# Q1 of a Strassen down projection made in two halves, and its weight sum T1 given tiles of its own

## The chip, the cores and the metric

The kernel runs on one core of a Trainium2 chip. The metric is the device time of one execution in microseconds (us). Names of engines: PE is the tensor engine (PEld its weight loads), DVE the vector engine, ACT the scalar engine, POOL the engine GpSimd, SP the sync engine, which issues most of the loads.

## The reference

A trunk of two layers on 512 tokens of 1024 features. Each layer has a token mixer, a cross-attention and an MLP, each followed by a layer norm of `alpha * x + sublayer(x)`. The change lies in the MLP, whose hidden width is 4096:

```python
def sq_relu_mlp(x, w1, b1, w2, b2):
    return jnp.square(jax.nn.relu(x @ w1 + b1)) @ w2 + b2
...
x = layer_norm(ALPHA * x + sq_relu_mlp(x, mlp_w1[i], mlp_b1[i], mlp_w2[i], mlp_b2[i]),
               ln_g[i, 2], ln_b[i, 2])
```

All data are float32.

## The kernel before

**Three matmuls for one.** Every operand of a matmul is split in a high part (a cast by ACT) and a low part (source minus high part, by DVE). `mm3` then issues three matmuls: high by high (line 198), high by the low part of the right side (199), and the low part of the left by the high part of the right (200). The names end in `h` and `l`.

**Quarters.** The 4096 hidden features are done in four quarters q of 1024. For q = 0, 1, 2 `up_down` makes the hidden tiles m = 0 to 7 (`s`: two tiles of four K tiles each, 128 hidden features per K tile) and then the down projection into `x`. In names "01" is layer 0, quarter 1. Quarter 3 has no Strassen products and is not touched. In quarters 1 and 2 the first six hidden tiles come from `up_pair`, which itself works with Strassen products (tiles `up`, `ub`, `utb`, `uta`, `ud`; PSUM `ua`, `ub`, `uc`), and tiles 6 and 7 from `feat_tile`, as do all eight in quarter 0.

**The down projection** is a Strassen product (Winograd's form) of the hidden block matrix, a11, a21 (K tiles 0 to 3, tokens 0 to 255 and 256 to 511), a12, a22 (K tiles 4 to 7), with the weights b11, b12, b21, b22 (512 by 512 each). Seven products stand on PE in this order: `u` = a11·b11, `f` = Q1·T1, `m2` = a12·b21, then onto `u` Q2·T2 and Q3·T3, onto `f` Q4·b22, onto `u` a22·T4. Here Q1 = a21 − a22, Q2 = −(a11 − a21) − a22, and the T are sums of weight blocks. Each product is 24 matmuls: 2 token tiles × 4 K tiles × 3. `a21` and `a22` are overwritten, so Q1 must be made after all eight hidden tiles, as the code stands.

**Weights.** `load` brings a block as two tiles of 128x1024 (pool `rawd`, six tiles) by SP. `onto_w` adds another block from HBM onto such tiles with an accumulating DMA on POOL's queue. `weight_split` makes high and low parts in the pools `wh` and `wl` of five tiles each; a tile comes free when PE has done its last matmul with it. The same pools serve the up projection. `split` makes the parts of an activation block in the pool `hid`.

In the code before, one pair of tiles `b` holds first b11, then T1 = b11 + b12, then T2, then T4:

```python
b = load("b11", 0, 0)
w = weight_split(f"b11{n}", b)
onto_w(b, 1, 0)
product(u, L["M1"], w, True, onto(0, 0))
V.tensor_tensor(a21, a21, a22, ALU.subtract)
w = weight_split(f"t1{n}", b)
onto_w(b, 1, 2)
product(f, split(f"q1{n}", a21), w, True, onto(1, 1))
```

**What sets the order.** Each engine, and each queue of DMA issues (SP's and POOL's), works through its own list in order and stops at an instruction whose inputs or buffers are not ready. The lists are fixed when the program is built, from the order of the code and from the buffers of the pools; an instruction can stand far from its neighbours in the code.

Of the kernel before, what the change touches and what calls it, by code (L numbers as in the profile page):

```python
# [10 lines left out]
F32R = mybir.dt.float32r  # L11
AF = mybir.ActivationFunctionType
ALU = mybir.AluOpType
AX = mybir.AxisListType

P = 128
# [23 lines left out]
def f32(ap):  # L40
    return ap.bitcast(F32)
# [3 lines left out]
def trunk(ctx: ExitStack, tc: tile.TileContext, a: dict, out: bass.AP):  # L45
    nc = tc.nc
    V, A, G, T = nc.vector, nc.scalar, nc.gpsimd, nc.tensor
# [22 lines left out]
    scoped = {}  # L70
# [126 lines left out]
    def mm3(out_, l, r, start, stop, skip=False):  # L197
        T.matmul(out_, l[0], r[0], start=start, stop=False, skip_group_check=skip)  # L198
        T.matmul(out_, l[0], r[1], start=False, stop=False, skip_group_check=skip)  # L199
        T.matmul(out_, l[1], r[0], start=False, stop=stop, skip_group_check=skip)  # L200
        if later:
            tick(3 * max(r[0].shape[-1], 128) / 2400)
# [10 lines left out]
    def tok(t):  # L213
        return slice(t * P, (t + 1) * P)
# [125 lines left out]
    for q in range(4):  # L340
# [3 lines left out]
        for z in range(2):  # L344
            k = 2 * q + z
            ld(r[:, z], a["xT"][:, k])
            h, l = x0.k(k)
# [122 lines left out]
    for j, c in enumerate((5, 2, 6, 3, 7, None, None, None)):  # L470
# [4 lines left out]
        for q in range(2):  # L475
            h = 2 * hf + q
# [177 lines left out]
    for i in range(DEPTH):  # L654
# [120 lines left out]
        def split(name, src):  # L775

            h, l = [scoped["hid"].tile([P, 4, 256], F32R, tag="hid", name=f"{name}{p}") for p in "hl"]
            A.copy(h, src)
            V.tensor_tensor(l, src, f32(h), ALU.subtract)
            return h, l  # L780

        def weight_split(name, src):
            us = []
            for j, r in enumerate(src):
                h = wh_p.tile([P, WU], F32R, tag="wh", name=f"{name}h{j}")
                l = wl_p.tile([P, WU], F32R, tag="wl", name=f"{name}l{j}")
                A.copy(h, r)
                V.tensor_tensor(l, r, f32(h), ALU.subtract)  # L788
                us.append([z.rearrange("p (k m) -> p k m", m=512) for z in (h, l)])
            return us  # L790

        def product(ps, lhs, rhs, start, evac):

            for g in range(2):
                for k in range(4):
                    w = rhs[k // 2]
                    mm3(ps[g], tuple(z[:, k, tok(g)] for z in lhs), (w[0][:, k % 2], w[1][:, k % 2]), start=start and k == 0, stop=k == 3, skip=not start)
                evac(g, ps[g])
# [3 lines left out]
        def block(r, c):  # L802

            return xm.half(c, slice(256 * r, 256 * r + 256))

        def x_sums():


            def raw(r, c):
                z = scoped["hid"].tile([P, 4, 256], F32, tag="hid", name=f"xr{i}{r}{c}")  # L810
                h, l = block(r, c)
                V.tensor_tensor(z, f32(h), f32(l), ALU.add)
                return z

            def parts(name, src, pool_):
                if pool_ is act_p:
                    z = act_p.tile([P, 2, 4, 256], F32R, tag="act", name=f"x{name}{i}")
                    h, l = z[:, 0], z[:, 1]
                else:
                    h, l = [pool_.tile([P, 4, 256], F32R, tag="hid", name=f"x{name}{i}{p}") for p in "hl"]  # L820
                A.copy(h, src)
                V.tensor_tensor(l, src, f32(h), ALU.subtract)
                xq[name] = h, l

            r = {}

            def start():
                r[22], r[21] = raw(1, 1), raw(1, 0)

            def q3():  # L830
                r[11] = raw(0, 0)
                V.tensor_tensor(r[11], r[11], r[21], ALU.subtract)

            def q1():
                parts("q3", r[11], act_p)
                V.tensor_tensor(r[21], r[21], r[22], ALU.subtract)

            def q2():
                parts("q1", r[21], act_p)
                V.scalar_tensor_tensor(r[11], r[11], -1.0, r[22], ALU.mult, ALU.subtract)  # L840

            def q4():
                parts("q2", r[11], scoped["hid"])
                r[12] = raw(0, 1)

            def end():
                V.tensor_tensor(r[12], r[12], r[11], ALU.add)
                parts("q4", r[12], scoped["hid"])

            chain(3, 5, [start, q3, q1, q2, q4, end])  # L850
# [66 lines left out]
        def up_down(q, n):  # L917

            s = [act_p.tile([P, 4, S], F32, tag="act", name=f"s{n}{b}") for b in range(2)]

            def ev(m, ps):
                r = t2(f"r{n}{m}")
                A.activation(r, ps, AF.Relu, bias=b1[:, i, 8 * q + m : 8 * q + m + 1], scale=1.0)
                A.activation(s[m // 4][:, m % 4], r, AF.Square)

            first = 0  # L930
            if q == 0:
                feat_first(f"h{n}", 4, lambda m: a["w1"][i, m], xm, ev)
                first = 4
                assert not later
                b2 = raw_p.tile([P, D], F32, tag="raw", name=f"b2{i}")
                ld(b2, a["b2"][i : i + 1, :].broadcast_to([P, D]))
                for t in range(NT):
                    V.scalar_tensor_tensor(x[t], x[t], ALPHA, b2, ALU.mult, ALU.add)
            a11, a21 = s[0][:, :, :256], s[0][:, :, 256:]
            a12, a22 = s[1][:, :, :256], s[1][:, :, 256:]  # L940
            L, R = {}, {}

            def load(name, hf, j):
                z = [scoped["rawd"].tile([P, WU], F32, tag="rawd", name=f"{name}{n}{z}") for z in range(2)]
                for w in range(2):
                    ld(z[w], a["w2"][i, q, hf, j + w])
                return z

            def first_blocks():
                L["M1"] = split(f"a11{n}", a11)  # L950
                V.tensor_tensor(a11, a11, a21, ALU.subtract)
                L["M7"] = split(f"q3{n}", a11)

            if q == 0:
                first_blocks()
                x_sums()
            for m in range(first, KC, 2):
                if m // 2 in STRASSEN_UP[q]:
                    up_pair(q, m, n, s[m // 4])
                else:  # L960
                    for z in range(2):
                        ev(m + z, feat_tile(f"h{n}{m + z}", a["w1"][i, 8 * q + m + z], xm, aux_p, "aux"))
                        last_product()
                if m == 4 and first == 0:
                    first_blocks()

            def onto(row, hf, op=ALU.add):
                def evac(g, ps):
                    z = x[2 * row + g][:, hf_cols(hf)]
                    V.tensor_tensor(z, z, ps, op)  # L970

                return evac

            def banks(name, p, tag):
                return [p.tile([P, 512], F32, tag=tag, name=f"{name}{n}{g}") for g in range(2)]

            u, f, m2 = banks("u", acc_p, "acc"), banks("f", acc_p, "acc"), banks("m2", tmp_p, "tmp")
            def onto_w(z, hf, j):

                for w in range(2):  # L980
                    G.dma_start(z[w], a["w2"][i, q, hf, j + w], accum_op=ALU.add)  # L981

            b = load("b11", 0, 0)
            w = weight_split(f"b11{n}", b)
            onto_w(b, 1, 0)
            product(u, L["M1"], w, True, onto(0, 0))
            V.tensor_tensor(a21, a21, a22, ALU.subtract)
            w = weight_split(f"t1{n}", b)
            onto_w(b, 1, 2)
            product(f, split(f"q1{n}", a21), w, True, onto(1, 1))  # L990
            b21 = load("b21", 0, 2)
            l12 = split(f"a12{n}", a12)
            product(m2, l12, weight_split(f"b21{n}", b21), True, onto(0, 0))
            t3 = load("t3", 1, 0)
            onto_w(t3, 1, 2)
            V.scalar_tensor_tensor(a11, a11, -1.0, a22, ALU.mult, ALU.subtract)
            w = weight_split(f"t2{n}", b)
            onto_w(b, 0, 2)
            product(u, split(f"q2{n}", a11), w, False, onto(0, 1, ALU.subtract))
            product(u, L["M7"], weight_split(f"t3{n}", t3), False, onto(1, 1, ALU.subtract))  # L1000
            b22 = load("b22", 1, 2)
            V.tensor_tensor(a12, a12, a11, ALU.add)
            product(f, split(f"q4{n}", a12), weight_split(f"b22{n}", b22), False, onto(0, 1))
            product(u, split(f"a22{n}", a22), weight_split(f"t4{n}", b), False, onto(1, 0))
# [15 lines left out]
        for q in range(3, 4):  # L1020
            n = f"{i}{q}"
            hid = Act(f"h{n}")
# [95 lines left out]
```

## Time and profile before

| | us |
|---|---|
| three runs | 1203.59, 1208.24, 1210.43 (median 1208.24) |
| profiled execution, own time | 1205.39 |
| its span, first to last instruction | 1203.5 |
| PE busy | 1184.3 (98%) |
| DVE busy | 847.3 (70%) |
| ACT busy | 616.2 (51%) |

The profiled execution is one more execution, with the profiler on. "Busy" of PE includes overlapping matmuls, so it does not say that PE runs at its best; what a place costs is read from the start times of matmuls there. The granted clock is a share of 2.4 GHz: 1.00 is the upper level, and a value between 0.5 and 1 means that part of the stretch ran at 1.2 GHz.

### The profile page before, as it was taken

To read this page: it belongs to the slowest core of one execution; us is meant where nothing else is said; L and a number is where in the kernel's file an instruction comes from. 1 tells how busy PE (TensorE), PEld (TensorE's weight loads), DVE (VectorE), ACT (ScalarE), POOL (GpSimd) and SP (SyncE) were. 2 spreads that over 40 slices of the span, in tenths; PEclk is the share of its full clock that TensorE was granted. 3 is DMA by queue.
4 is the path that set the end of the run, shared out by engine and by line. 5 is a ranking of instruction groups with operands and counts; after the bars stand their busy time and mean duration, and the time that the engine had idled before them with its cause. 6 is when DMAs were issued, how large, how long until landed. Compare 5 with 4: busy or idle time off the path is not lost.

```text
span 1203.5 us, 16624 instructions
## 1 busy us (share of the span) xinstructions
PE 1184.3 (98%) x6537; PEld 1027.5 (85%) x6537; DVE 847.3 (70%) x1173; ACT 616.2 (51%) x912; POOL 61.1 (5%) x99
## 2 busy tenths in 40 slices
PE   9999999999999999999999999999999999999997
PEld 7888898889889879879888889998987988978886
DVE  6774466585549798597775599775979869767336
ACT  6585774234423655656646434562365574654530
POOL 0211000000000000100100000000000010010000
PEclk9999999999999999999999999999999999999999
DMA  7344258633172643936745355637364583764311
GB/s 273 91 137 121 88 158 268 203 108 96 61 210 88 141 88 129 217 78 214 171 117 198 123 193 193 191 90 210 93 135 88 167 200 71 227 143 105 104 53 70
DMA packets 50974, 171.83 MB, mean 143 GB/s; under 512 B 6336, under 2 KB 6604, under 8 KB 50896
## 3 DMA queue, kind: packets, MB, share of 16 engines
q1 hardware_dynamic: 42960, 142.96, 36.6%
q0 software_dynamic: 7936, 27.81, 13.3%
q8 instruction: 51, 0.84, 0.3%
q14 instruction: 27, 0.22, 0.1%
HBM read 164.43 MB, written 6.31 MB: 142 GB/s over the span
## 4 chain that ended last, share of the span: by engine, by line
PE 82%; DVE 7%; DMA 4%; ACT 3%; issue 3%; POOL 0%; DVEq 0%; POOLq 0%; ACTq 0%; SPq 0%
PE h L198 5%; PE h L199 5%; PE h L200 5%; PE m L198 3%; PE m L199 3%; PE m L200 3%; PE u L198 3%; PE u L199 3%; PE u L200 3%; PE ao L200 2%; PE ao L198 2%; PE ao L199 2%; PE f L200 2%; PE q L199 2%; PE q L198 2%
## 5 line engine op out<-in xcount | busy, mean ns | idle before, releaser
L162 DVE TENSOR_TENSOR wl<-raw,wh 128x1024 fp32r<-128x1024 f32 x151 | 184.1, 1221 | 152.5 <-ACT wh L161 150.4
L161 ACT CAST wh<-raw 128x1024 fp32r<-128x1024 f32 x151 | 157.9, 1048 | 220.6 <-PE h L199 51.8
L981 POOL DMA_DIRECT2D b<-in_w x36 | 31.6, 879 | 281.0 <-DVE b1100l L788 62.3
L981 POOL DMA_DIRECT2D t<-in_w x12 | 10.7, 942 | 644.4 <-DMA t<-in_w 415.9
L249 ACT ACTIVATE rs<-mv,eps_t 128x1 f32<-128x1 f32 x24 | 7.1, 294 | 53.3 <-DVE mv L247 53.3
L198 PE MATMUL h<-xm00h,wh 128*128 128x512 f32 (+1 forms) x96 | 34.2, 356 | 0.0
L198 PE MATMUL h<-xm10h,wh 128*128 128x512 f32 (+1 forms) x96 | 34.2, 356 | 0.0
L198 PE MATMUL h<-xm11h,wh 128*128 128x512 f32 (+1 forms) x96 | 34.1, 355 | 0.0
L198 PE MATMUL h<-xm01h,wh 128*128 128x512 f32 (+1 forms) x96 | 34.1, 355 | 0.0
L199 PE MATMUL h<-xm10l,wh 128*128 128x512 f32 (+1 forms) x96 | 34.1, 355 | 0.0
L199 PE MATMUL h<-xm00l,wh 128*128 128x512 f32 (+1 forms) x96 | 34.1, 355 | 0.0
L200 PE MATMUL h<-xm00h,wl 128*128 128x512 f32 (+1 forms) x96 | 34.0, 354 | 0.0
L200 PE MATMUL h<-xm10h,wl 128*128 128x512 f32 (+1 forms) x96 | 34.0, 354 | 0.0
L200 PE MATMUL h<-xm11h,wl 128*128 128x512 f32 (+1 forms) x96 | 34.0, 354 | 0.0
L199 PE MATMUL h<-xm01l,wh 128*128 128x512 f32 (+1 forms) x96 | 34.0, 354 | 0.0
L200 PE MATMUL h<-xm01h,wl 128*128 128x512 f32 (+1 forms) x96 | 34.0, 354 | 0.0
L199 PE MATMUL h<-xm11l,wh 128*128 128x512 f32 (+1 forms) x96 | 34.0, 354 | 0.0
L677 ACT ACTIVATE pr<-s,nm 128x256 f32<-128x256 f32 x32 | 14.9, 471 | 12.5 <-DVE nm L672 9.7
L198 PEld LDWEIGHTS h<-xm01h,wh 128*128 128x128 f32 x96 | 18.2, 189 | 2.5
L200 PEld LDWEIGHTS h<-xm00h,wl 128*128 128x128 f32 x96 | 18.2, 189 | 2.5
L199 PEld LDWEIGHTS h<-xm11l,wh 128*128 128x128 f32 x96 | 18.2, 189 | 2.5
L200 PEld LDWEIGHTS h<-xm10h,wl 128*128 128x128 f32 x96 | 18.1, 189 | 2.5
(1588 smaller groups left out, 4154.4 us busy)
## 6 DMA issues: line engine op xcount, KB each, us to landing
raw<-in_w SPq DMA_DIRECT2D x64, 512.0 KB, 3.8
b<-in_w SPq DMA_DIRECT2D x36, 512.0 KB, 4.6
b<-in_w POOLq DMA_DIRECT2D x36, 512.0 KB, 5.8
raw<-in_w_q SPq DMA_DIRECT2D x24, 512.0 KB, 4.2
up<-in_w SPq DMA_DIRECT2D x24, 512.0 KB, 3.9
raw<-in_w_ao SPq DMA_DIRECT2D x16, 512.0 KB, 3.7
t<-in_w SPq DMA_DIRECT2D x12, 512.0 KB, 5.2
t<-in_w POOLq DMA_DIRECT2D x12, 512.0 KB, 9.0
```

The lines of the kernel that those rows point to most:

```text
L161: A.copy(h, r)
L162: V.tensor_tensor(l, r, f32(h), ALU.subtract)
L198: T.matmul(out_, l[0], r[0], start=start, stop=False, skip_group_check=skip)
L199: T.matmul(out_, l[0], r[1], start=False, stop=False, skip_group_check=skip)
L200: T.matmul(out_, l[1], r[0], start=False, stop=stop, skip_group_check=skip)
L249: A.activation(rs, mv[:, 1:2], AF.Sqrt, bias=eps_t, scale=1.0)
L677: A.activation(pr[:, ms], ps[:, ms], AF.Exp, bias=nm[:, t_ : t_ + 1], scale=1.0, accum_out=sm[:, t_ : t_ + 1])
L981: G.dma_start(z[w], a["w2"][i, q, hf, j + w], accum_op=ALU.add)
```

## The change

T1 gets its own pair of tiles `b`, loaded with b11 a second time, so that its accumulation need not wait for b11's parts. Q1 is made in two halves of two K tiles each, as soon as the hidden tiles of a half are there by the code's order, and stands in the code ahead of the splits of the weights. All else is the same.

```diff
+            def q1_part(ks):
+
+                if "M5" not in L:
+                    L["M5"] = [scoped["hid"].tile([P, 4, 256], F32R, tag="hid", name=f"q1{n}{p}") for p in "hl"]
+                h, l = (z[:, ks] for z in L["M5"])
+                d = a21[:, ks]
+                V.tensor_tensor(d, d, a22[:, ks], ALU.subtract)
+                A.copy(h, d)
+                V.tensor_tensor(l, d, f32(h), ALU.subtract)
+
             for m in range(first, KC, 2):
...
+            q1_part(slice(0, 2))
+            q1_part(slice(2, 4))
+            l21 = L["M5"]
...
-            b = load("b11", 0, 0)
-            w = weight_split(f"b11{n}", b)
+            b11, b = load("b11", 0, 0), load("t1", 0, 0)
             onto_w(b, 1, 0)
+            w = weight_split(f"b11{n}", b11)
             product(u, L["M1"], w, True, onto(0, 0))
-            V.tensor_tensor(a21, a21, a22, ALU.subtract)
-            w = weight_split(f"t1{n}", b)
+            w1 = weight_split(f"t1{n}", b)
             onto_w(b, 1, 2)
-            product(f, split(f"q1{n}", a21), w, True, onto(1, 1))
+            product(f, l21, w1, True, onto(1, 1))
```

On DVE, in quarter 01, from the low part of T1's second tile to that of b21's second tile. `q101l` is the low part of Q1, `s010` and `s011` the two tiles of hidden features, `xin` the result. Before:

```order
L788 TENSOR_TENSOR t101l1_4728<-b11011_4683,t101h1_4727 128x1024
L788 TENSOR_TENSOR b2101l0_4772<-b21010_4763,b2101h0_4771 128x1024
L987 TENSOR_TENSOR s010_4225<-s010_4225,s011_4226 128x4x256
L970 TENSOR_TENSOR xin0_2050<-xin0_2050,u010_4676 128x512
L996 SCALAR_TENSOR_TENSOR s010_4225<-s010_4225,s011_4226 128x4x256
L779 TENSOR_TENSOR q101l_4734<-s010_4225,q101h_4733 128x1024
L970 TENSOR_TENSOR xin1_2052<-xin1_2052,u011_4677 128x512
L779 TENSOR_TENSOR a1201l_4768<-s011_4226,a1201h_4767 128x1024
L788 TENSOR_TENSOR b2101l1_4776<-b21011_4764,b2101h1_4775 128x1024
```

The same place with the change:

```order
L788 TENSOR_TENSOR t101l1_4746<-t1011_4702,t101h1_4745 128x1024
L963 TENSOR_TENSOR s010_4232<-s010_4232,s011_4233 128x2x256
L965 TENSOR_TENSOR q101l_4684<-s010_4232,q101h_4683 128x512
L788 TENSOR_TENSOR b2101l0_4786<-b21010_4777,b2101h0_4785 128x1024
L963 TENSOR_TENSOR s010_4232<-s010_4232,s011_4233 128x2x256
L1008 SCALAR_TENSOR_TENSOR s010_4232<-s010_4232,s011_4233 128x4x256
L965 TENSOR_TENSOR q101l_4684<-s010_4232,q101h_4683 128x512
L983 TENSOR_TENSOR xin0_2050<-xin0_2050,u010_4691 128x512
L779 TENSOR_TENSOR a1201l_4782<-s011_4233,a1201h_4781 128x1024
L983 TENSOR_TENSOR xin1_2052<-xin1_2052,u011_4692 128x512
L788 TENSOR_TENSOR b2101l1_4790<-b21011_4778,b2101h1_4789 128x1024
```

The first half of Q1 stands ahead of b21's first low part, the second half behind it and ahead of the additions to `xin`. On ACT, in the same quarter, from T1's second cast on (`r016`, `r017` are the ReLUs of the last two hidden tiles). Before:

```order
L787 CAST t101h1_4727<-b11011_4683 128x1024
L928 ACTIVATE s011_4226<-r016_4622 128x512
L910 COPY s011_4226<-ua014_4484 128x256
L912 ACTIVATE s011_4226<-s011_4226,b1_985 128x512
L913 ACTIVATE s011_4226<-s011_4226 128x512
L787 CAST b2101h0_4771<-b21010_4763 128x1024
L927 ACTIVATE r017_4673<-h017_4648,b1_985 128x512
L928 ACTIVATE s011_4226<-r017_4673 128x512
L778 CAST q101h_4733<-s010_4225 128x1024
L787 CAST b2101h1_4775<-b21011_4764 128x1024
```

With the change:

```order
L787 CAST t101h1_4745<-t1011_4702 128x1024
L928 ACTIVATE s011_4233<-r016_4629 128x512
L910 COPY s011_4233<-ua014_4491 128x256
L912 ACTIVATE s011_4233<-s011_4233,b1_985 128x512
L913 ACTIVATE s011_4233<-s011_4233 128x512
L964 CAST q101h_4683<-s010_4232 128x512
L787 CAST b2101h0_4785<-b21010_4777 128x1024
L927 ACTIVATE r017_4680<-h017_4655,b1_985 128x512
L928 ACTIVATE s011_4233<-r017_4680 128x512
L778 CAST a1201h_4781<-s011_4233 128x1024
L964 CAST q101h_4683<-s010_4232 128x512
L787 CAST b2101h1_4789<-b21011_4778 128x1024
```

The first half's cast stands ahead of b21's, the second half's behind a12's. On POOL's queue, the accumulating DMAs of quarter 01 (`t3010` and `t3011` hold T3; the other pair holds T1, T2 and T4 in turn). Before:

```order
L981 DMA t3010_4805<-in_w2 128x1024
L981 DMA t3011_4806<-in_w2 128x1024
L981 DMA b11010_4682<-in_w2 128x1024
L981 DMA b11011_4683<-in_w2 128x1024
L981 DMA b11010_4682<-in_w2 128x1024
L981 DMA b11011_4683<-in_w2 128x1024
```

With the change:

```order
L994 DMA t1010_4701<-in_w2 128x1024
L994 DMA t1011_4702<-in_w2 128x1024
L994 DMA t3010_4819<-in_w2 128x1024
L994 DMA t3011_4820<-in_w2 128x1024
L994 DMA t1010_4701<-in_w2 128x1024
L994 DMA t1011_4702<-in_w2 128x1024
```

T1's pair moves from the second to the first place, and T3's stands between T1's and T2's. On SP's queue b11's pair and T1's are loaded around the units of the last two hidden tiles, ahead of b21's, and T3's pair moves from behind b21's to a place behind the next quarter's first three weight loads, where it takes over b11's tiles.

## Rows read from the trace of the kernel before

**Rows 1.** The page, its first lines: busy us, share of the span, instructions.

```profile
span 1203.5 us, 16624 instructions
PE 1184.3 (98%) x6537; PEld 1027.5 (85%) x6537; DVE 847.3 (70%) x1173; ACT 616.2 (51%) x912; POOL 61.1 (5%) x99
```

**Rows 2.** Waits of PE: us in total, times, longest us.

```profile
PE f L198 <- ACT q112h L778: 2.3, 1, 2.3
```

**Rows 3.** Timeline of PE, quarter 01: start us, duration us, first matmuls of products.

```profile
500.35 0.28 PE L200 MATMUL ua<-xm01h,utb014wl 128*128 128x256 f32 x1
...
505.93 0.39 PE L198 MATMUL u<-b1101h,a1101h 128*128 128x512 f32 x1
...
518.63 0.39 PE L198 MATMUL m<-b2101h,a1201h 128*128 128x512 f32 x1
...
524.07 0.39 PE L198 MATMUL u<-t201h,q201h 128*128 128x512 f32 x1
```

**Rows 4.** Stretches from `u` to `m2`, PE alone: us, busy, clock, DMA, GB/s.

```profile
424.47:437.20 12.73, 11.50 (x50) 1.00 0.56 124
...
1065.30:1081.25 15.95, 13.07 (x49) 0.89 0.63 132
sum 79.23, PE 70.47; mean PE 11.74
```

**Rows 5.** Quarter 12: stretch of `f` (PE, PEld, DVE, ACT, POOL, clock), a matmul.

```profile
1073.20:1081.30 8.10, 7.50 (x25) 5.69 (x26) 6.55 (x8) 4.77 (x5) 0.00 (x0) 0.79 0.38 119
...
1075.96 0.63 PE L200 MATMUL f<-t112h,q112l 128*128 128x512 f32 x1
```

**Rows 6.** Timeline of ACT, quarter 01; in brackets the idle time before.

```profile
504.31 1.05 ACT L787 CAST t101h<-b 128x1024 fp32r<-128x1024 f32 x1 [0.82 <-DMA b<-in_w]
...
507.48 1.03 ACT L787 CAST b2101h<-b 128x1024 fp32r<-128x1024 f32 x1
...
509.13 0.63 ACT L928 ACTIVATE s<-r 128x512 f32<-128x512 f32 x1
511.06 1.05 ACT L778 CAST q101h<-s 128x1024 fp32r<-128x1024 f32 x1 [1.29 <-DVE s L987]
```

**Rows 7.** Timeline of DVE, quarters 00 and 01.

```profile
457.80 0.69 DVE L880 TENSOR_TENSOR ut010a<-up 128x512 f32<-128x512 f32 x1
458.40 0.69 DVE L878 TENSOR_TENSOR ut010b<-ut010b,up 128x512 f32<-128x512 f32 x1
...
494.20 2.35 DVE L788 TENSOR_TENSOR b1101l<-b,b1101h 128x1024 fp32r<-128x1024 f32 x2
```

**Rows 8.** Timeline of the queues SP and POOL, quarter 01: issues of DMAs.

```profile
479.39 0.33 SPq L92 DMA_DIRECT2D raw<-in_w  x1
...
496.96 0.87 POOL L981 DMA_DIRECT2D b<-in_w  x1 [0.25 <-issue]
...
507.03 0.90 POOL L981 DMA_DIRECT2D b<-in_w  x1 [1.58 <-DVE t101l L788]
```

**Rows 9.** DMA issues of the whole span: KB each, median us to landing.

```profile
t<-in_w SPq DMA_DIRECT2D x12, 512.0 KB, 5.2
t<-in_w POOLq DMA_DIRECT2D x12, 512.0 KB, 9.0
```

**Rows 10.** Stretches of quarters 00 and 01 (columns as in rows 5).

```profile
409.20:440.50 31.30, 30.07 (x132) 24.23 (x131) 31.23 (x30) 19.78 (x23) 4.25 (x5) 1.00 0.51 95
497.70:502.90 5.20, 5.20 (x30) 4.55 (x29) 0.00 (x0) 1.04 (x2) 0.13 (x1) 1.00 0.93 175
480.00:500.00 20.00, 19.88 (x145) 18.72 (x144) 12.75 (x15) 13.26 (x21) 3.53 (x4) 1.00 0.97 263
```

**Rows 11.** Timeline of quarter 00: DVE, and PE's first matmul of Q2·T2.

```profile
431.24 1.22 DVE L779 TENSOR_TENSOR q100l<-s,q100h 128x1024 fp32r<-128x1024 f32 x1
...
439.25 1.22 DVE L779 TENSOR_TENSOR q200l<-s,q200h 128x1024 fp32r<-128x1024 f32 x1
...
442.64 0.39 PE L198 MATMUL u<-t200h,q200h 128*128 128x512 f32 x1
```

## The prediction

> **What bounds the kernel now.** The page's first lines come first: TensorE (PE) is busy for 1184.3 of the 1203.5 us and VectorE (DVE) for 70% [rows 1]. So time can only come from places where PE stands, or from a lower clock. The waits of PE come next: the longest is the one of `f`, the second product of a down projection, for `q112h`, the high part of Q1. In each of the six quarters (two layers, q = 0 to 2; "01" is layer 0, quarter 1) `f` waits twice, for Q1's high part from ScalarE (ACT) and for its low part from DVE; one of these twelve rows is shown, the longest [rows 2].
>
> A wait row gives only what the trace calls idle, so I measure the loss from starts. In quarter 01 the third product starts at 518.63 and the fourth at 524.07: an undisturbed product of 24 matmuls takes 5.44 us, 0.227 us each [rows 3]. From the first matmul of the first product (`u`) to that of the third (`m`) two products should take 10.88 us. The six stretches add up to 79.23 us [rows 4], and 79.23 − 6 × 10.88 = **13.95 us** is lost around Q1. Quarter 00 loses 1.85, quarter 12 loses 15.95 − 10.88 = 5.07, and the other four the rest, 1.76 each. There the wait is 2.3 us, and after it the granted clock of the stretch falls to 0.79: a matmul lasts 0.63 us where 0.39 is usual [rows 3], so the chip was at its lower level, 1.2 instead of 2.4 GHz, for a part of `f` [rows 5]. That is a second price of the same wait.
>
> Why Q1 is late is read from ACT's and DVE's rows of quarter 01. T1's second tile is cast at 504.31, when its accumulating DMA lands. Behind it in ACT's line stand the hidden tiles' last steps, then the cast of b21 at 507.48, the last ReLU, the last square (509.13, 0.63 long), and only after DVE's subtraction Q1's cast at 511.06 [rows 6]. PE wants Q1 at 505.93 + 5.44 = 511.37. So a late DMA holds ACT, and ACT holds Q1.
>
> **The change, part by part.** *T1 in tiles of its own.* Before, T1's accumulation can be issued only when b11's low part has been made (494.20 + 2.35 = 496.6 for the second tile [rows 7]); it is issued at 496.96, with the wait ended [rows 8]. Now T1's copy of b11 is loaded into other tiles, in SyncE's (SP) line right behind the load issued at 479.39 [rows 8]. Three issues of 0.33 and a load of 5.2 us end at about 485.6; two issues of 0.9 and an accumulation of at most about 9.0, the slowest kind in the table [rows 9], give 496. The casts of T1 then no longer wait for a DMA, but for the weight tiles that PE gives back when it ends the pair's last product, near 500.6 [rows 3]: T1's second cast starts some 3 us before 504.31. The work between T1's second cast and b21's (3.2 us by rows 6) then ends near 504; with Q1's first half, 0.6 of cast and 0.7 of subtraction by half-size rows, it ends near 505.4. So b21's cast is held only by the weight tile that PE frees at 505.93. From b21's start to the end of the last square took 2.28 us [rows 6], which gives 508.2.
>
> *Q1 in halves.* The first half (K tiles 0 and 1) needs the hidden tiles 0, 1, 4 and 5 alone, and is done near 506, 5 us before 511.37. For the second half: subtraction at 508.2 (0.69 for a 512-wide row [rows 7]), a cast of a12 ahead of it on ACT until 509.3, its own cast of about 0.6, and on DVE the sum for Q2 (1.13) and the low part (0.69): done at about 510.7. PE reaches K tile 2 six matmuls into `f`, at 512.7, and wants its low part at 513.2. So there is a lead of 2.5 us, and the wait is gone in quarters 01, 02, 11 and 12. What is late next is b21's second tile and the T2 sum; on the same reckoning both stand some 3 us ahead of PE.
>
> *The price of the halves.* DVE does four instructions of 512 for two of 1024. Rows 7 give 0.60 from start to start for the small ones (457.80 to 458.40) and 1.13 for the large ones (two in 2.35, ends overlapping), so 4 × 0.60 − 2 × 1.14 = 0.12 us per quarter on DVE, and two casts more on ACT. Where DVE has slack this is hidden: in quarter 01 it does nothing at all from 497.7 to 502.9 [rows 10]. The Trainium skill speaks against the split: "VectorE: DVE Perf Modes", section "The TRN2 errata — SBUF-src ops pay a fixed extra latency per instruction", says that every instruction pays a fixed extra, so that many small tiles cost more than one large one, and its fp32 formula has 0.69 us for 512 and 1.22 for 1024, as the durations in rows 7 also say. By durations alone a split would cost 2 × 0.69 − 1.22 = 0.16, twice per quarter, and 1.9 us over six quarters if nothing hid it; with that in the sum in place of the 0.5 below it would be 1193.3. I take the start-to-start price, since the next instruction starts before the former one's end.
>
> *The first quarters, 00 and 10.* Here T1 came early before, too; DVE is the limit, busy for 31.23 of 31.30 us from 409.2 to 440.5 [rows 10]. It gains nothing from an earlier DMA, only from order. Q1's low part ended at 431.24 + 1.22 = 432.46; now the sum for Q2 (1.13) and one addition to x (0.60) come behind it, and with 0.12 more work it ends near 430.9 [rows 11]. PE would start `f` at 424.47 + 5.44 = 429.91 and want K tile 2's low part at 431.7. Later Q2's low part ends at 440.47 + 0.12 = 440.6; PE, 1.85 us earlier than 442.64, wants it with its third matmul at 441.2 [rows 11]. The leads are 0.9 and 0.6 us: thin, but enough.
>
> *The queues.* Two more loads of 512 KB per quarter, twelve in all. T3's load loses its free tiles and waits for b11's; T3 is wanted only for the fifth product. On GpSimd's (POOL) line T3's accumulation now stands between T1's and T2's. The interleaved start of `f` on PE is gone; it costs nothing, since the same 24 matmuls remain.
>
> *Sum.* 1205.4 (the profiled execution's own time; span 1203.5) − 13.95 = 1191.4. For new small waits in up-projection pairs and first quarters I add 0.5 us, an estimate between nothing and the 1.9 above: **about 1192 us**. The profiled execution is 2.85 us faster than the median of the three runs (1208.24, from 1203.59 to 1210.43), so against the median this is −1.3%. I do not add the 2.85, since a DMA that lands late, with the clock loss behind it, is what differs from quarter to quarter here, and this change takes it off the path.
>
> **The rivals.** *1. DVE gives back the first quarters.* If DVE runs 2.5 us later there than I reckon, the 1.85 us of 00 and of 10 come back: 1192 + 3.7 = 1195.7. For it speaks its 31.23 of 31.30 us, against it that order alone frees 1.7 us ahead of Q1.
>
> *2. T2 is late.* T3's load may start only when b11's low parts are done, 496.6 [rows 7], lands 5.2 us later near 502, and its two accumulations go out ahead of T2's. T2's second tile is then issued near 505.4 where the old row has 507.03 [rows 8], but four accumulations are in the air at once. If that doubles the landing of 9.0 us [rows 9], T2 is there at 523.4, its cast and low part 2.3 us later, and PE, which wants it 1.36 us after 511.37 + 2 × 5.44 = 522.25, stands for 2.1 us in four quarters: 1192 + 8.4 = 1200.4. With 9.0 us there is no wait.
>
> *3. The wait only changes its name.* `f` might wait for T1's low part or the last hidden tile instead, for as long as before: 1205. Against it speaks that the second half has a lead of 2.5 us.
>
> *4. The added loads make T1 late, and the kernel slower.* From 480 to 500 the DMA engines are busy for a share of 0.97 at 263 GB/s [rows 10]; the added 1.05 MB take 4.0 us of that, ahead of b21 and of the next weights. T1's second tile after 503.5 (501 and the lead of 2.5) would bring a wait back, and from 504.31 on, the old landing, each microsecond costs one more in four quarters; 508 would give 1205.4 − 3.7 + 4 × 3.7 = 1216.5. It decides from a landing near 506.7, where (3.7 + 6) / 4 = 2.4 us per quarter eat the gain and 6 us more; that is ten later than my 496. Against it: T1's chain starts 17.5 us earlier (479.4 for 497.0). The Trainium skill's rule behind this is in "Trainium Kernel Development and Optimization", section "Key Constraints": DMAs issued from SP's and POOL's queues run on the same 16 engines and interleave; the share of 0.97 agrees that the stretch is full.
>
> **How the numbers follow.** The forecast has 0.70 (1188 to 1196), rival 1 0.08, rival 2 0.10, rival 3 0.07, rival 4 0.05. A difference of 0.5% (6 us) is about what a measurement of this kernel can tell from none: faster is below 1202.2. That sums to 0.88 for faster; some of rival 2 lies at the edge, so 0.86, 0.09 and 0.05. The range runs from 1188 (the shortest run was 1.8 us under the profiled one) to 1200, which leaves out rivals 3 and 4 and the end of 2.
>
> **What would show it.** In the new trace `f` has no row among PE's waits; from `u` to `m` it takes 10.9 to 11.0 us in all six quarters, and quarter 12 keeps its clock. T1's casts wait for PE, not for a DMA. A PE wait at the T2 product would show rival 2, one of `f` for T1 rival 4, one at Q2's low part in 00 and 10 rival 1. The forecast is wrong if a DMA share near 1 makes T1 land after 504.

## The result, and the profile after

The changed kernel takes 1191.4 us (median of four runs, 1190.97 to 1193.63), the kernel before 1208.03 (four runs, 1203.59 to 1210.43). The ratio is 0.987, with a 95% interval from 0.984 to 0.990. The profiled execution took 1193.63 us with a span of 1191.9.

The page of the changed kernel, its first lines, as in [rows 1]:

```profile
span 1191.9 us, 16669 instructions
PE 1180.2 (99%) x6537; PEld 1028.2 (86%) x6537; DVE 847.5 (71%) x1185; ACT 616.9 (52%) x918; POOL 61.8 (5%) x99
```

Its waits of PE, all but those under 0.5 us, as in [rows 2]; no row of `f` is left:

```profile
PE warm L312 <- POOL zero L309: 1.3, 1, 1.3
PE po L200 <- DVE d1l L208: 1.1, 1, 1.1
PE po L198 <- ACT d1h L207: 1.0, 2, 0.8
```

The stretches from `u` to `m2`, PE alone (us, busy, clock, DMA share, GB/s), three of six and the sum, as in [rows 4]:

```profile
424.53:435.41 10.88, 10.88 (x49) 1.00 0.59 131
503.77:514.65 10.88, 10.88 (x49) 1.00 1.01 229
...
1059.01:1069.89 10.88, 10.88 (x49) 1.00 0.93 205
sum 65.28, PE 65.28; mean PE 10.88
```

65.28 is exactly 6 × 10.88: of the 13.95 us lost around Q1 nothing is left, and the clock is 1.00 in quarter 12 as well. ACT in quarter 01, from T1's first cast on, as in [rows 6]:

```profile
496.84 1.05 ACT L787 CAST t101h<-t 128x1024 fp32r<-128x1024 f32 x1 [2.07 <-PE h L199]
...
498.38 1.05 ACT L787 CAST t101h<-t 128x1024 fp32r<-128x1024 f32 x1
...
503.74 1.05 ACT L787 CAST b2101h<-b 128x1024 fp32r<-128x1024 f32 x1 [0.72 <-PE h L199]
...
505.41 0.63 ACT L928 ACTIVATE s<-r 128x512 f32<-128x512 f32 x1
```

T1's first cast waits for PE, which gives back the weight tile, and no longer for a DMA; the second waits for nothing. In this profile quarter 01 begins 2.16 us earlier than before (`u` at 503.77 instead of 505.93). With these 2.16 us added, T1's second cast stands at 500.54 where it was at 504.31, and the last square ends at 508.20, as forecast (508.2).

The span is 11.6 us shorter, while 13.95 came back in the quarters. The missing 2.3 lie mainly in one place, layer 1's attention. First the changed kernel's profile, PE, PEld, DVE, ACT, POOL and the clock of 731 to 746 and the cast of query weights there:

```profile
731.00:746.00 15.00, 13.15 (x95) 12.73 (x95) 11.85 (x26) 4.51 (x10) 0.00 (x0) 0.89 0.40 144
737.65 1.05 ACT L161 CAST wh<-raw 128x1024 fp32r<-128x1024 f32 x1 [3.30 <-DMA raw<-in_w_q]
```

and the same stretch in a later profile of the same kernel (after_third below):

```profile
731.00:746.00 15.00, 14.35 (x121) 14.12 (x121) 13.69 (x30) 5.20 (x12) 0.00 (x0) 1.00 0.55 197
```

One transfer landed late, PE stood here for 0.8 us for `d1h` and 1.1 us for `d1l`, and the clock fell. The other two profiles of this kernel have spans of 1190.0 and 1189.0 and a clock of 1.00 here.

### The profile page after: what moved, and what is told of

Its sections match the earlier page's. It is cut to its first block, busy times and chain, and to the rows that moved or that the text cites. A ratio compares the mean times of both kernels' runs of the same rounds, so it can differ in the third digit from the quotient of the medians.

```text
span 1191.9 us, 16669 instructions
## 1 busy us (share of the span) xinstructions
PE 1180.2 (99%) x6537; PEld 1028.2 (86%) x6537; DVE 847.5 (71%) x1185; ACT 616.9 (52%) x918; POOL 61.8 (5%) x99
## 4 chain that ended last, share of the span: by engine, by line
PE 94%; DVE 2%; ACT 1%; DMA 1%; issue 0%; SPq 0%; DVEq 0%; ACTq 0%
PE h L198 6%; PE h L199 6%; PE h L200 6%; PE u L198 4%; PE u L200 4%; PE u L199 4%; PE m L200 3%; PE m L198 3%; PE m L199 3%; PE ao L198 2%; PE ao L200 2%; PE ao L199 2%; PE q L199 2%; PE q L198 2%; PE q L200 2%; PE ua L198 2%
## 5 line engine op out<-in xcount | busy, mean ns | idle before, releaser
L994 POOL DMA_DIRECT2D t<-in_w x48 | 42.4, 918 | 914.7 <-DMA t<-in_w 506.2
L912 ACT ACTIVATE s<-s,b 128x512 f32<-128x512 f32 x24 | 17.4, 723 | 6.5 <-DVE s L906 6.1
L200 PEld LDWEIGHTS h<-xm11h,wl 128*128 128x128 f32 x96 | 18.1, 189 | 2.5
```

Of the source, the lines that this page charges most:

```text
L912: A.activation(z, z, AF.Relu, bias=b1[:, i, 8 * q + m + c : 8 * q + m + c + 1], scale=1.0)
```

## The experiments

In the table, "lost" is the sum over the six quarters of the time from `u` to `m2` less 10.88, in the one profiled execution; medians and ratios are those of separate runs.

| kernel | median us | ratio to before | lost, 00 and 10 | lost, 01, 02, 11, 12 |
|---|---|---|---|---|
| before (first profile) | 1208.03 | 1 | 1.85, 1.82 | 1.82, 1.62, 1.77, 5.07 |
| before_again | one run, 1211.41 | | 1.85, 1.84 | 3.52, 2.00, 4.63, 5.29 |
| after_again | 1191.47 | 0.987 (0.9847 to 0.9893) | 0, 0 | 0, 0, 0, 0 |
| t1_own | 1196.01 | 0.9906 (0.9885 to 0.9927) | 1.84, 1.84 | 0.24, 0.24, 0.24, 0.25 |
| q1_early | 1202.22 | 0.9957 (0.9938 to 0.9975) | 0, 0 | 3.72, 0.56, 1.44, 1.94 |
| whole_early | 1208.09 | 1.0005 (0.999 to 1.0019) | 3.43, 3.43 | 0.24 each |
| halves_late | 1191.93 | 0.9859 (0.9827 to 0.9891) | 0.18, 0.15 | 0, 0, 0, 0 |
| load_twice | 1199.45 | 0.9918 (0.9888 to 0.9947) | 0, 0 | 2.07, 0, 0, 0 |
| kv_sooner | 1192.65 | 0.9865 (0.9829 to 0.99) | 0, 0 | 0, 0, 0, 0 |
| mixed | 1192.25 | 0.987 (0.985 to 0.9891) | 0, 0 | 0.24, 0.25, 0.24, 0.25 |
| lean | 1191.84 | 0.9864 (0.9843 to 0.9885) | 0, 0 | 0, 0, 0, 0 |
| after_third | 1191.73 | 0.9867 (0.9843 to 0.9891) | 0, 0 | 0, 0, 0, 0 |

What a kernel loses behind `m2` does not stand in the table; it is told with the kernel. The theory behind them: two causes, T1's late DMA in quarters 01, 02, 11 and 12 and the order on DVE in 00 and 10. The rivals give all to one of them.

**The changed kernel again (after_again).** No edit.

> The changed kernel unaltered, for comparison with the other kernels on this chip. Theory: from u to m2 it takes 10.9 us in all six quarters again, ratio to the kernel before 0.987. The stand of PE between 736 and 745 in layer 1 (3.6 us against the kernel before) comes from one transfer of query weights that landed late: if that is chance, PE's waits there change from profile to profile; if it belongs to the change, they are there again at about 2 us.

The quarters came out as expected. The wait of `po` for ACT's `d1h` was gone and that for DVE's `d1l` there again (1.0), with no fall of the clock: the late transfer is not there in every execution. The small wait is no mark of the change, since the kernel before has it too (0.8 us for `d1h` in the first profile, 1.0 for `d1l` in before_again).

**T1's tiles alone (t1_own).** Against the kernel before:

```diff
-            b = load("b11", 0, 0)
-            w = weight_split(f"b11{n}", b)
+            b11, b = load("b11", 0, 0), load("t1", 0, 0)
             onto_w(b, 1, 0)
+            w = weight_split(f"b11{n}", b11)
```

> Only T1 in tiles of its own; Q1 is made in one piece at its old place. Theory (two causes): T1's casts no longer wait for a transfer, so in quarters 01, 02, 11 and 12 f gets Q1's high part in time and waits only for the low part, about 0.45 us (u to m2 11.3 us); quarters 00 and 10 keep their loss of 1.85 us, since the order on DVE stays. Lost in all about 3.7 + 1.8 = 5.5 of the 13.95 us, a ratio near 0.993. Rival A (the order of Q1 alone matters): 01, 02 and 11 still lose 1.7, a ratio of 0.998. Rival B (the tiles alone matter): 0.987, with 00 and 10 at 10.9 us.

Stretches of t1_own from `u` to `m2` (columns as above):

```profile
424.52:437.24 12.72, 11.48 (x50) 1.00 0.53 135
505.60:516.72 11.12, 11.12 (x49) 1.00 0.82 188
```

So it went: nothing in 00 and 10, all but 0.24 of the loss in the other four, 9.3 of 13.95 us. The remaining wait is 0.24 instead of 0.45 because the built order of PE takes the two high-part matmuls of the next K tile ahead of the one that waits for Q1's low part; I had left that out.

**Q1's halves alone (q1_early).** Against the changed kernel:

```diff
-            b11, b = load("b11", 0, 0), load("t1", 0, 0)
+            b = load("b11", 0, 0)
+            w = weight_split(f"b11{n}", b)
             onto_w(b, 1, 0)
-            w = weight_split(f"b11{n}", b11)
```

> Only Q1 in two early halves; T1 shares b11's tiles as before. Theory (two causes): quarters 00 and 10 lose nothing. In the others T1 lands as late as before, near 1.6 us ahead of u, but Q1's second half is then done about when PE comes to its third K tile: 0 to 0.3 us lost in 01, 02 and 11, and 1 to 2 in quarter 12. Lost in all 1.5 to 3 us, a ratio of 0.989. Rival A (the order alone matters): 0.987 and no quarter above 11.0 us. Rival C (late T1 undoes the halves): 01, 02 and 11 still lose 1.7 and 12 about 5, a ratio of 0.996.

ACT and PE of q1_early in quarter 01, where `u` starts at 504.14:

```profile
504.00 1.05 ACT L787 CAST t101h<-b 128x1024 fp32r<-128x1024 f32 x1 [1.37 <-DMA b<-in_w]
...
511.83 0.61 ACT L964 CAST q101h<-s 128x512 fp32r<-128x512 f32 x1
...
512.50 0.50 PE L198 MATMUL f<-t101h,q101h 128*128 128x512 f32 x1 [1.40 <-ACT q101h L964]
```

00 and 10 came out at nothing, as the theory has it; the others are a miss, and nearer to rival C. I had taken T1's landing as fixed at 1.62 us ahead of `u` [rows 3, 6]. Here it came at nearly the same time (504.00 for 504.31), while PE, with quarter 00 repaired, came 1.8 us earlier: 0.14 us ahead of `u`. Q1's second half is late, PE stands 1.4 us, and the clock falls after it (0.88 over the stretch). The halves move Q1 forward by some 2 us, and a late T1 takes that back. A second wait came up that I had not listed: `u` of the fifth product waits for DVE's addition to `x` (PE's waits of 1.1 us in two quarters together and 0.8 in one). DVE, put behind by ACT's late line, comes late to it; in quarter 02 it works without a break from 592.73 until past that addition. With this the stretch from the fourth product's start to the sixth's took 2.9 us too long in the four quarters.

**Both, with Q1 in one piece (whole_early).** Against the changed kernel:

```diff
-            q1_part(slice(0, 2))
-            q1_part(slice(2, 4))
+            q1_part(slice(0, 4))
```

> T1 in tiles of its own and Q1 at its early place, but in one piece. Theory (the halves matter for Q1's low part): in 01, 02, 11 and 12 the order of ACT and DVE is that of the kernel with T1's tiles alone, so about 0.45 us is lost in each; in 00 and 10, where the sums for the next quarter now stand behind Q1, about 0.5 us each. Lost in all 3 us, a ratio near 0.990. Rival D (the place alone matters, the halves nothing): 0.987 and 10.9 us in all quarters. Rival E (without halves the place does nothing): 1.85 us lost in 00 and 10, a ratio of 0.993.

The four quarters 01, 02, 11 and 12 lose 0.24, as t1_own does. In 00 and 10 it went far worse than in any of the cases. PE and ACT of whole_early in quarter 00:

```profile
439.50 0.50 PE L198 MATMUL m<-b2100h,a1200h 128*128 128x512 f32 x1 [3.03 <-ACT a1200h L778]
```

```profile
435.15 1.05 ACT L787 CAST t200h<-t 128x1024 fp32r<-128x1024 f32 x1 [2.51 <-PE f L200]
436.51 1.04 ACT L787 CAST t300h<-t 128x1024 fp32r<-128x1024 f32 x1 [0.30 <-PE f L200]
437.46 1.04 ACT L821 CAST xq40h<-xr 128x1024 fp32r<-128x1024 f32 x1
438.41 1.04 ACT L778 CAST a1200h<-s 128x1024 fp32r<-128x1024 f32 x1
```

`f` itself takes only the 0.24 us longer that the other four quarters lose too. With the whole Q1 put first, the sums for the next quarter's up projection (`xq20l`, `xr`) slide behind it on DVE, the cast of `xq40h` behind them on ACT, and a12's cast behind T2's second and T3's first cast, which wait for tiles that PE frees only late in `f`. The third product wants a12 right behind `f`. So PE stands 3.0 us, then 0.9 more for a12's low part, and after it the granted clock is 0.50:

```profile
436.50:439.50 3.00, 0.00 (x0) 1.00 0.23 64
441.00:447.00 6.00, 5.61 (x13) 0.50 0.88 150
```

The third product then takes 9.51 instead of 5.44 us: 3.43 + 4.07 = 7.5 us in quarter 00 and as much in 10, 15 us, more than T1's tiles bring. ACT took up a12's cast at 438.41, behind the three casts above, though the last square of its source had ended at 427.46. The Trainium skill, "PSUM — Partial Sum Buffer", section "Engine vs sequencer instructions", says that the queues of ScalarE, VectorE and GpSimd are strict first-in, first-out, and ACT's rows agree.

**Q1's halves at the old place (halves_late).** Against the changed kernel:

```diff
-            q1_part(slice(0, 2))
-            q1_part(slice(2, 4))
-            l21 = L["M5"]
...
             w1 = weight_split(f"t1{n}", b)
             onto_w(b, 1, 2)
+            q1_part(slice(0, 2))
+            q1_part(slice(2, 4))
+            l21 = L["M5"]
```

> T1 in tiles of its own and Q1 in halves, but at its old place in the code, behind T1's split. In quarters 01, 02, 11 and 12 the engines' order is almost that of the changed kernel, so 10.9 us from u to m2. Theory (in 00 and 10 the place decides): the second half's low part stands behind b21's second and one more addition on DVE and ends near 432.9 where PE wants it at 431.8, so about 1.1 us is lost in each of these two, a ratio of 0.989. Rival (with halves the place does nothing): 10.9 us everywhere, 0.987.

The place is worth 0.33 us in all by the profile, which no timing shows; I had said 2.2. So the rival is nearly right: in 00 and 10 the halves bring back nearly all of the 3.7 us, at either place. DVE's row of the second half in quarter 00 of halves_late:

```profile
432.15 0.68 DVE L965 TENSOR_TENSOR q100l<-s,q100h 128x512 fp32r<-128x512 f32 x1
```

It ends at 432.83, 7.88 us behind `u` (424.95). I had reckoned 432.9 with `u` at 424.47, 8.4 us behind, so it came half a microsecond sooner. PE wants it at 430.39 + 8 × 0.227 = 432.21 and works two matmuls ahead (0.45) meanwhile, so the loss is 0.18.

**T1 loaded twice (load_twice).** Against the changed kernel:

```diff
             b11, b = load("b11", 0, 0), load("t1", 0, 0)
+            for w in range(2):
+                ld(b[w], a["w2"][i, q, 0, w])
```

> The changed kernel with each T1 block loaded twice into the same tiles, so that T1's sum and all loads behind it on SP's queue start 5 to 6 us later and twelve more loads use the DMA engines; the result is the same. Theory (the added load is hidden, with over 3 us to spare): T1's second tile lands near 500 instead of 495, up to 2 us behind the weight tile that its cast waits for now, which the lead of Q1's second half takes up: 10.9 to 11.2 us from u to m2, a ratio of 0.987 to 0.988. Rival 4 of the prediction (the DMA engines are full and T1 lands late): 13 us or more in four quarters, a ratio of 0.995 or above.

POOL and ACT of load_twice in quarter 01 (`u` at 504.24):

```profile
490.65 0.90 POOL L994 DMA_DIRECT2D t<-in_w  x1 [0.65 <-issue]
```

```profile
504.06 1.05 ACT L787 CAST t101h<-t 128x1024 fp32r<-128x1024 f32 x1 [3.75 <-DMA t<-in_w]
```

and its waits of PE:

```profile
PE u L198 <- DVE xp L983: 2.8, 1, 2.8
PE f L198 <- ACT q101h L964: 1.4, 1, 1.4
```

It is 8 us slower than the changed kernel, between theory and rival. Of the four quarters one pays for a late T1: its accumulation took 13.4 us, not 9.0. There T1's second cast started 0.18 us ahead of `u`, 2.25 later than the 2.43 ahead which the prediction had as its bound (503.5 with `u` at 505.93), and 2.07 us were lost. In q1_early the same casts started 0.75, 1.63 and 2.11 us behind that bound in 02, 11 and 12, and 0.56, 1.44 and 1.94 us were lost: the bound holds to 0.2 us, and a later T1 is paid one for one while the clock holds. In 01 of q1_early, where the clock fell, 2.29 us behind the bound cost 3.72.

In quarter 11 it is T2's first tile that comes late:

```profile
993.41 1.05 ACT L787 CAST t211h<-t 128x1024 fp32r<-128x1024 f32 x1 [5.11 <-DMA t<-in_w]
```

```profile
994.49 1.23 DVE L788 TENSOR_TENSOR t211l<-t,t211h 128x1024 fp32r<-128x1024 f32 x1 [3.77 <-ACT t211h L787]
```

DVE, in its order, then adds `u` to `x` late, and the fifth product, which writes on the same `u`, waits 2.8 us. So the added load is hidden in the changed kernel, but a second one of its size is not.

**Keys and values sooner (kv_sooner).** Against the changed kernel:

```diff
-                            kv_back(x[t])
+                            for _ in range((1, 3, 0, 0)[t]):
+                                kv_back(x[t])
```

> The changed kernel with the last four loads of the spilled keys and values issued with the second pair, some 30 us earlier, so that they don't stand among the query weights of layer 1. An attempt at a faster version. Theory (one late transfer of query weights holds PE between 728 and 745): the waits of PE there go, 1 to 2 us less than the changed kernel, a ratio of 0.986. Rival (the weights next to the new place are late instead, or another wait takes its place): 0.987 or above.

No gain: waits of 0.8 for query weights and 0.8 for `d1h` stand where the others stood, and the median is 0.7 us above that of halves_late beside it. The rival holds; these waits of about 1 us are left as they are.

**The kernel before, a second profile (before_again).** No edit.

> The kernel before, for a second profile. Theory: quarters 00 and 10 lose 1.8 us again (their order on DVE is fixed and no transfer is late), while in the other four the loss goes with T1's landing and differs from execution to execution, between 1.6 and 5 us; the sum lies between 11 and 19 us. Rival (the 5 us of quarter 12 belong to that quarter): the same six numbers as in the first profile.

Its stretches from `u` to `m2`, as in [rows 4]:

```profile
425.30:438.03 12.73, 11.48 (x49) 1.00 0.48 124
507.26:521.66 14.40, 11.44 (x50) 1.00 0.56 117
590.02:602.90 12.88, 11.51 (x50) 1.00 0.65 137
906.11:918.83 12.72, 11.49 (x49) 1.00 0.51 124
987.19:1002.70 15.51, 12.83 (x50) 0.89 0.60 131
1071.06:1087.23 16.17, 13.07 (x50) 0.89 0.60 131
sum 84.41, PE 71.82; mean PE 11.97
```

00 and 10 are as in the first profile to 0.02 us; 01 and 11 now lose 3.52 and 4.63, near to the 5.29 of 12. The sum is 84.41 − 65.28 = 19.13 us, 0.13 above the range I gave, and the span 6 us longer. ACT's second cast of T1 in 01 and 11:

```profile
507.38 1.05 ACT L787 CAST t101h<-b 128x1024 fp32r<-128x1024 f32 x1 [3.08 <-DMA b<-in_w]
...
987.25 1.05 ACT L787 CAST t111h<-b 128x1024 fp32r<-128x1024 f32 x1 [0.88 <-DMA b<-in_w]
```

In 01 T1 landed 0.12 us behind `u`, 1.74 later against it than in the first profile, and the loss is 3.52 − 1.82 = 1.70 larger: here, at a clock of 1.00, a late landing is paid one for one. In 11 it came 1.71 later against `u`, and with the fall of the clock the loss is 2.86 larger. In 12 T1's second cast stood 0.04 us behind `u` in the first profile and 0.27 in this one, so that quarter lost most both times. The old kernel's spread fits this: in one comparison of 19 runs it took 1202.5 to 1211.95 us, the changed kernel beside it 1191.2 to 1192.71 in five.

**Halves in 00 and 10 alone (mixed), tiles in the other four alone (lean), and the changed kernel on the same chip (after_third).** Against the changed kernel, first mixed, then lean:

```diff
-            q1_part(slice(0, 2))
-            q1_part(slice(2, 4))
+            for ks in (slice(0, 2), slice(2, 4)) if q == 0 else (slice(0, 4),):
+                q1_part(ks)
```

```diff
-            b11, b = load("b11", 0, 0), load("t1", 0, 0)
-            onto_w(b, 1, 0)
+            b11 = load("b11", 0, 0)
+            b = b11 if q == 0 else load("t1", 0, 0)
+            if q:
+                onto_w(b, 1, 0)
             w = weight_split(f"b11{n}", b11)
+            if q == 0:
+                onto_w(b, 1, 0)
```

> T1 in tiles of its own; Q1 early, in halves in quarters 00 and 10 and in one piece in the other four. Theory (in one piece only the order of ACT and DVE in 00 and 10 is ruined): 10.9 us from u to m2 in 00 and 10, 11.12 in the others, 1.0 us lost in all: about 1192.5 us, a ratio within 0.1% of the changed kernel's. Rival (the piece also costs elsewhere, in the up projections behind it): above 1196 us.

> Q1 early in halves everywhere; T1 in tiles of its own in quarters 01, 02, 11 and 12 alone, so four of the twelve added loads go. Theory (00 and 10 need only the order): nothing lost in any quarter, 1191.4 us as for the changed kernel, or less by what four loads cost. Rival (T1's own tiles are needed in 00 and 10 too, once Q1 is early): about 1.8 us lost in each, 1195 us.

> The changed kernel unaltered once more, for comparison with the two kernels on the same chip: 1191.4 us, 10.9 us from u to m2 in all quarters.

All three came out as expected. Mixed from `u` to `m2`, quarters 00 and 01 and the sum:

```profile
424.37:435.25 10.88, 10.88 (x50) 1.00 0.48 111
503.61:514.73 11.12, 11.12 (x49) 1.00 0.94 199
...
sum 66.26, PE 66.26; mean PE 11.04
```

The medians, 1192.25, 1191.84 and 1191.73, can't be told apart. Each part is needed in its own quarters: the halves in 00 and 10, T1's tiles in the rest. There one early piece costs only the 0.24 us that t1_own loses too. Lean does the same with four loads fewer; no version tried beats the changed kernel by more than its spread.

## Why the prediction was right

**The bound and the size.** 13.95 us lost around Q1, all given back: shown, 65.28 = 6 × 10.88. The time forecast, 1192, and the −1.3% stand beside 1191.4 and 0.987.

**The landing of T1.** The prediction took 9.0 us for "at most"; rows 9 give a median, of T3's accumulations. In the changed kernel T1's second accumulation of quarter 01, issued at 484.15, took longer:

```profile
t<-in_w POOLq DMA_DIRECT2D x1, 512.0 KB, 12.1
```

It landed at 496.2, 7.6 us ahead of `u`, where the forecast had 496 with `u` at 505.93, 9.9 ahead. This did no harm: the landing is 2.2 us ahead of T1's second cast, and b21's cast behind it is held by PE (503.74, above) as forecast. But the distance to the bound is 5.1 us, not 7.5.

**The cause in 01, 02, 11 and 12.** That a late DMA holds ACT, and ACT holds Q1, is shown by t1_own (1.6 to 5.1 us become 0.24 when T1 alone is early) and by before_again (the loss follows the landing).

**The cause in 00 and 10.** That order alone helps there, and not an earlier DMA, is shown by t1_own (nothing) and by q1_early and lean (all); halves_late adds that of the order nearly all is the halves, and next to nothing their place in the code. Leads measured in the changed kernel, from DVE's rows and PE's starts:

```profile
429.93 0.69 DVE L965 TENSOR_TENSOR q100l<-s,q100h 128x512 fp32r<-128x512 f32 x1
...
439.74 1.22 DVE L779 TENSOR_TENSOR q200l<-s,q200h 128x1024 fp32r<-128x1024 f32 x1
```

```profile
429.97 0.39 PE L198 MATMUL f<-t100h,q100h 128*128 128x512 f32 x1
```

```profile
441.30 0.39 PE L200 MATMUL u<-t200h,q200l 128*128 128x512 f32 x1
```

Q1's second low part ends at 430.62 and PE wants it eight matmuls into `f`, at 429.97 + 8 × 0.227 = 431.78: a lead of 1.16, forecast 0.9. Q2's ends at 440.96, wanted at 441.30: 0.34, forecast 0.6. Rival 1 would have begun there; it did not. In quarter 01 the lead of 2.5 for Q1's second low part came out to the tenth:

```profile
507.82 0.69 DVE L965 TENSOR_TENSOR q101l<-s,q101h 128x512 fp32r<-128x512 f32 x1
```

ends at 508.51, and `f` starts at 503.77 + 5.44 = 509.21 and wants it at 511.02.

**The price of the halves.** Twelve more instructions, and DVE is busy 0.2 us longer (847.3 to 847.5), where six times 0.12 was forecast. (The working reads 1.13 us and then uses 1.14; with 1.13 it is 0.14. The 1.22 us for 1024 stand in rows 11, not in rows 7.) The fixed cost per instruction, which the Trainium skill ("VectorE: DVE Perf Modes", section "The TRN2 errata — SBUF-src ops pay a fixed extra latency per instruction") holds against small tiles, is there in the durations (0.69 us for 512, 1.22 for 1024), but it cost PE nothing that a run shows.

**The added 0.5 us** for new waits was not seen in the quarters; the one wait of size found elsewhere was a late transfer of one execution. **The 2.85 us** between the profiled execution and the median of the kernel before were rightly not added, as far as two profiles tell: the one that lost 13.95 us took 1205.39 and the one that lost 19.13 took 1211.41, and less their losses they come to 1191.4 and 1192.3.

**Rival 4** was given 0.05, to decide from a landing 10 us later than 496. Load_twice and q1_early show its bound of 503.5 right. Its price was too high: it counted the old loss in full from 504.31 on, 3.3 us for the landing of load_twice in 01, and 2.07 were lost, since the halves still bring Q1 forward. And the distance was overrated: T1's second accumulation went out 6.5 us later than in the changed kernel,

```profile
484.15 0.90 POOL L994 DMA_DIRECT2D t<-in_w  x1 [0.41 <-issue]
```

and that was enough, since it then took 13.4 us where I had allowed 9.0. **Rival 2** (T2 late behind T3) did not come: T2's second cast does wait for its DMA in 02, 11 and 12 of the changed kernel, but in 11, where it waits longest (3.8 us), T2's low part is still 4.4 us ahead of PE. T2 is what fails next, as load_twice shows in quarter 11.

What the prediction did not see is that the halves are needed for more than Q1's own speed: in one piece, the same early place in the code costs 15 us in 00 and 10 by moving a12's cast behind a wait for PE.

## What to carry to other kernels

When PE is near 100% busy, measure the loss from start to start of equal products; the twelve idle rows of `f` before add up to only 8.7 of the 13.95 us. Follow a late operand back through the in-order engine to the first instruction that waits for something outside, and repair that, since what stands behind it is only queued; then check what each moved instruction puts behind a wait for PE. Two parts of one change can have their own places: by medians beside the kernel before, T1's tiles alone bring 11.4 us, the halves alone 5.2, and both 16.0.

## What the runs showed of the hardware that was not expected

**The clock after a stand.** PE stood for 2.3 to 3.0 us ahead of `f` or `m2` in several places, at a clock of 1.00, and in most of them the clock then was at its lower level. In before_again, quarters 12, 11 and 01 in that order (PE alone):

```profile
1081.00:1085.00 4.00, 4.00 (x11) 0.57 0.08 8
996.00:999.00 3.00, 2.62 (x7) 0.50 0.14 52
515.20:518.20 3.00, 2.39 (x9) 1.00 0.27 111
```

Ahead of them PE had waited 2.51, 2.30 and 2.36 us for Q1's high part. The same wait cost the clock in two quarters and not in the third, where 3.5 us were lost instead of 4.6 and 5.3. So a wait of this length has a price that varies by 1 to 2 us. A shorter one can cost the clock as well: PE waited 1.40 us for Q1's high part in quarter 01 of q1_early and 1.35 in that of load_twice, with nearly the same starts, and the clock behind it (PE alone, first q1_early) was:

```profile
513.00:516.00 3.00, 2.86 (x8) 0.66 0.23 90
513.00:516.00 3.00, 2.87 (x13) 1.00 1.06 229
```

From `u` to `m2` 3.72 us were lost in the one and 2.07 in the other. What decides it, no run here shows.

**An accumulating DMA's time to land.** The same 512 KB on POOL's queue took 7.35 us in quarter 01 before (issued at 496.96, cast at 504.31, [rows 6, 8]), 12.1 in the changed kernel and 13.4 in load_twice (490.65 to 504.06). The DMA engines were nearly as full each time, with a share of 0.89, 0.99 and 0.95 in the three stretches, but they moved 162 GB/s before, 283 in the changed kernel and 284 in load_twice, so more other data went beside it:

```profile
490.00:504.00 14.00, 14.00 (x76) 12.14 (x76) 7.23 (x8) 5.94 (x7) 1.79 (x2) 1.00 0.95 284
```

Whether that is why it took so much longer, no run settles.
